# First output chunks in spare PSUM banks, and the last memory head's samples on TensorE

## The chip, the cores and the metric

One core of a Trainium2 chip runs the kernel as one program. The metric is the device time of an execution in microseconds (us), lower is better. A core has five engines that work side by side, each through its own queue in order: PE (TensorE, matmul into PSUM), DVE (VectorE), ACT (ScalarE), POOL (GpSimd) and SP (which here issues the DMAs). PSUM is the memory that matmuls write; this kernel divides it into eight banks of 128 partitions by 512 float32 values.

## What is computed

One inference step of a small decoder with two layers and model width 1024, for a prompt of 256 tokens and 8 samples of one token each, which share the weights; the kernel treats them as 264 columns. Each sublayer f is wrapped as x + norm(f(norm(x))), with an RMS norm whose factor r is one number per column. Layer 0 mixes tokens with a Mamba-2 state-space mixer (SSD), layer 1 with dilated sliding-window attention. After the mixer each layer has cross-attention with 4 heads of 256 dimensions into 256 memory tokens, and a convolutional feed-forward network of width 2816:

```
def cross_attn(u, kv, w_q, w_o):
    n, t_len, _ = u.shape
    q = (u @ w_q).reshape(n, t_len, MEM_HEADS, MEM_HEAD_DIM)
    s = jnp.einsum('nthe,nmhe->nhtm', q, kv[:, :, 0].astype(q.dtype)).astype(jnp.float32) * (MEM_HEAD_DIM ** -0.5)
    p = jax.nn.softmax(s, axis=-1)
    o = jnp.einsum('nhtm,nmhe->nthe', p, kv[:, :, 1].astype(jnp.float32))
    return o.reshape(n, t_len, D_MODEL).astype(u.dtype) @ w_o
```

The prompt's memory keys and values are computed from the memory tokens by weights. Each of the 8 samples has its own memory keys and values, given as a cache (cache_mem_kv). Outputs are the new activations and all new states and caches.

## The kernel before, in words

Activations lie transposed: model dimension on the partitions in chunks of 128, the 264 columns along the free axis. Every weight product is made by `product` (line 771) one output chunk of 128 rows at a time. `wsplit` (757) loads a chunk of weights (tile raw), ACT rounds it to the faster matmul format (hi) and DVE subtracts to get the rest (lo); inputs are split in the same way (uhl). Each of the 8 contraction steps is three matmuls (hi with high input, hi with low input, lo with high input), 24 for a chunk of 8 steps, all into one PSUM accumulator. In `product` the accumulators are the tag "mm" with two banks; raw has four buffers, hi and lo three each.

The eight PSUM banks are divided by tags: mm 2 (products), s 2 (`small`, 716: sums of the norm, the prompt's attention), t 3 (`other`, 719: the samples' work and the state update), f 1 (the memory keys and values and some of the SSD).

A stage begins in `Post.finish` (897): the norm of the sublayer before gives r, then for each of 8 chunks the residual x is updated and split into the next input (`Pre.add`, 875), and its square is summed; `rstd` (801) turns the sum into the next r by a matmul with ones, two ACT operations and three of DVE. The product itself needs only the split input, but the eviction of a query, key, gate or up chunk multiplies by r, so it waits for it: `evac` (798) on DVE in the SSD's conv, the attention's qc and the feed-forward's cons (1679), where a gate chunk then has its convolution (gr, gy) and an up chunk is multiplied with its gate and split (mh, ml). Output products (w_out, xa_o, ffn_d) are evicted by ACT without r.

The memory attention is `xattn` (1313). For each head h it makes two query chunks, then calls `keys` (1348), `soft` (1366) of the head before, `scores` (1394, the prompt's part) and `values` (1381) of the head before. For the samples of one head, `caches` (1326) loads keys or values in four tiles (tag kv, KVB = 6 buffers) of two samples each. For each sample PE broadcasts the query (qs) or the probabilities (prs) over 128 partitions by one matmul into a t bank, and DVE multiplies each of the two halves of the sample's tile with it and sums along the free axis:

```
V.scalar_tensor_tensor(out=kv[:, i, :], in0=kv[:, i, :], scalar=1.0, in1=tq,
                       op0=ALU.mult, op1=ALU.mult, accum_out=a)
```

That is 16 DVE operations (kv<-kv,t in the profile) for the keys of a head and 16 for its values, 128 per layer. `mix` (1421) joins the prompt's result (matmuls s<-ppT,ld with the reloaded prompt values vn) and the samples' (os) into the split input of the output product.

`memkv` (1264) makes the prompt's memory keys and values of a layer in the f bank, stores them (o_memk, o_memv), and `xattn` loads them back. It is called "aside": its operations fill time beside other stages; layer 0's runs beside the output product of the SSD and into the first memory attention, layer 1's up to the second. `states` (1243) updates the SSD states of the samples during the first feed-forward, with t banks.

The order of the instructions on every queue is not that of the source. The program records all operations, and a planner (`Plan.run`, 364, `rank`, `latest` and `order`) lists them with costs of its own: six passes (PASSES) simulate the engines and correct the priorities by the latest times of the pass before; the order with the shortest simulated length is emitted. SPARE sets how early loads are due, SWITCH what a change of ACT's table costs in the choice. A buffer of a tag is given in the order of the source: a later tile of a tag can't have one before an earlier one. All instructions are issued in one line, 622, so the profile's groups are told apart by their tiles.

## Time and profile before

| | us |
|---|---|
| time, median of 3 runs | 1154.57 (1153.74 to 1155.39) |
| the profiled execution, its own time | 1153.77 |
| its span in the profile | 1152.0 |
| PE busy / DVE busy / ACT busy | 1036.8 / 893.9 / 643.8 |

The span is the time from the first to the last instruction that the profiler recorded; the execution's own time has 1.8 us around it. Busy times are those of one engine and overlap with the others'. Matmuls are pipelined: each has a duration of some 0.3 us, but one starts every 0.12 us or so, so the rate is read from the length of a run of them. The stages lie like this in the span (us): SSD 0 to 240, with its output product; first memory attention to 420; first feed-forward to 653; dilated attention to 820; second memory attention to 930; last feed-forward to the end.

### The profile page before, as it was taken

To read this page: it belongs to the slowest core of one execution; us is meant where nothing else is said; L and a number is where in the kernel's file an instruction comes from. 1 tells how busy PE (TensorE), PEld (TensorE's weight loads), DVE (VectorE), ACT (ScalarE), POOL (GpSimd) and SP (SyncE) were. 2 spreads that over 40 slices of the span, in tenths; PEclk is the share of its full clock that TensorE was granted. 3 is DMA by queue.
4 is the path that set the end of the run, shared out by engine and by line. 5 is a ranking of instruction groups with operands and counts; after the bars stand their busy time and mean duration, and the time that the engine had idled before them with its cause. 6 is when DMAs were issued, how large, how long until landed. Compare 5 with 4: busy or idle time off the path is not lost.

```text
span 1152.0 us, 21202 instructions
## 1 busy us (share of the span) xinstructions
PE 1036.8 (90%) x7895; PEld 982.8 (85%) x7895; DVE 893.9 (78%) x2060; ACT 643.8 (56%) x1273; POOL 60.7 (5%) x142
## 2 busy tenths in 40 slices
PE   5899978889998797999999899999884969999995
PEld 5898967889988686999999889989883859999995
DVE  7989999975889889998754675474897776777544
ACT  6896665655643487785544543455542455555542
POOL 0210210000000001221000000000000000000000
PEclk9999989989999798999999999998995989999998
DMA  7335444756799686887566776587398326777761
GB/s 261 128 111 174 158 142 170 258 189 219 263 335 305 233 315 217 306 293 243 173 215 210 251 261 260 192 308 269 128 299 290 118 92 219 284 265 271 271 183 52
DMA packets 80599, 257.20 MB, mean 223 GB/s; under 512 B 16952, under 2 KB 21848, under 8 KB 79344
## 3 DMA queue, kind: packets, MB, share of 16 engines
q1 hardware_dynamic: 80496, 255.85, 64.8%
q8 instruction: 62, 1.02, 0.3%
q14 instruction: 41, 0.34, 0.1%
HBM read 238.70 MB, written 44.34 MB: 246 GB/s over the span
## 4 chain that ended last, share of the span: by engine, by line
PE 63%; DVE 21%; ACT 6%; DMA 5%; issue 4%; SPq 1%; DVEq 0%; ACTq 0%
PE mm L622 48%; PE f L622 6%; PE s L622 6%; DVE kv L622 4%; DVE lo L622 3%; PE t L622 3%; DMA o_sssm<-sto 2%; ACT hi L622 2%; DVE xs L622 1%; DVE hif L622 1%; DVE yv L622 1%; DVE r L622 1%; DVE kvo L622 1%; DVE mix L622 1%; DVE x L622 1%
## 5 line engine op out<-in xcount | busy, mean ns | idle before, releaser
L622 PE MATMUL mm<-uhl,hi 128*128 128x264 f32 x2960 | 574.5, 292 | 41.5 <-ACT uhl L622 14.8
L622 PEld LDWEIGHTS mm<-uhl,hi 128*128 128x128 f32 x2960 | 470.6, 192 | 52.6 <-ACT uhl L622 16.6
L622 DVE TENSOR_TENSOR lo<-raw,hi 128x1024 fp32r<-128x1024 f32 (+1 forms) x283 | 338.7, 1199 | 149.5 <-ACT hi L622 145.7
L622 PE MATMUL mm<-uhl,lo 128*128 128x264 f32 x1480 | 425.0, 288 | 0.7 <-DVE lo L622 0.7
L622 ACT CAST hi<-raw 128x1024 fp32r<-128x1024 f32 (+1 forms) x283 | 292.0, 1033 | 233.5 <-PE mm L622 209.6
L622 PEld LDWEIGHTS mm<-uhl,lo 128*128 128x128 f32 x1480 | 282.6, 191 | 1.7 <-DVE lo L622 1.1
L622 PE MATMUL mm<-mh,lo 128*128 128x264 f32 x352 | 100.1, 284 | 0.0
L622 PE MATMUL mm<-mh,hi 128*128 128x264 f32 x352 | 100.0, 284 | 0.0
L622 PE MATMUL mm<-ml,hi 128*128 128x264 f32 x352 | 99.8, 283 | 0.0
L622 DVE SCALAR_TENSOR_TENSOR kv<-kv,t 128x256 f32<-128x256 f32 x256 | 88.9, 416 | 8.4 <-PE t L622 8.3
L622 PEld LDWEIGHTS mm<-mh,lo 128*128 128x128 f32 x352 | 66.3, 188 | 0.0
L622 PEld LDWEIGHTS mm<-ml,hi 128*128 128x128 f32 x352 | 66.2, 188 | 0.0
L622 PEld LDWEIGHTS mm<-mh,hi 128*128 128x128 f32 x352 | 66.2, 188 | 0.0
L622 PE MATMUL f<-mh,hi 128*128 128x256 f32 x128 | 38.4, 300 | 11.1 <-ACT kvo L622 5.6
L622 ACT ACTIVATE sto<-t,sdt 128x128 f32<-128x128 f32 x128 | 37.3, 394 | 13.4 <-DMA o_sssm<-sto 11.7
L622 DVE SCALAR_TENSOR_TENSOR gy<-gr,ld,gy 128x255 f32<-128x255 f32 x88 | 42.3, 480 | 1.1 <-ACT gy L622 1.0
L622 PE MATMUL f<-hi,mh 128*128 128x256 f32 x128 | 38.4, 300 | 3.2 <-ACT kvo L622 3.2
L622 PE MATMUL f<-ml,hi 128*128 128x256 f32 x128 | 37.4, 292 | 3.8 <-DVE ml L622 3.8
L622 ACT CAST mh<-gy 128x264 fp32r<-128x264 f32 x44 | 18.3, 416 | 39.7 <-DVE gy L622 39.7
L622 PE MATMUL f<-hi,ml 128*128 128x256 f32 x128 | 38.1, 298 | 2.3 <-ACT kvo L622 2.3
L622 POOL COPY pst<-gr 128x2 f32<-128x2 f32 x44 | 23.7, 538 | 304.4 <-DVE gr L622 304.4
L622 PE MATMUL f<-lo,mh 128*128 128x256 f32 x128 | 38.0, 297 | 0.2 <-DVE lo L622 0.2
(284 smaller groups left out, 1717.8 us busy)
## 6 DMA issues: line engine op xcount, KB each, us to landing
raw<-ffn_gu SPq DMA_DIRECT2D x88, 512.0 KB, 4.3
raw<-w_in SPq DMA_DIRECT2D x40, 512.0 KB, 3.5
kv<-cmk SPq DMA_DIRECT2D x32, 512.0 KB, 5.9
kv<-cmv SPq DMA_DIRECT2D x32, 512.0 KB, 5.6
raw<-ffn_d SPq DMA_DIRECT2D x32, 512.0 KB, 3.7
o_sc<-cache SPq DMA_DIRECT2D x16, 1022.0 KB, 8.4
raw<-w_qkv SPq DMA_DIRECT2D x18, 512.0 KB, 3.9
rawf<-state SPq DMA_DIRECT2D x16, 512.0 KB, 4.4
```

What stands on the lines that cost most here:

```text
L622: f(*a, **k)
```

## The change

Three things change. First, `product` takes the bank of its accumulator from a list, head, as long as that has entries: two mm banks, then banks of t or s. The list is set at the start of the program (SSD: five entries), of the dilated attention (five), of the first feed-forward (four: mm, mm, s, s) and of the last (five), and emptied in the memory attention. Entries with 'f' also use the weight buffers of `memkv` (tags rawf, hif, lof, two buffers each). Second, for head 3 (ONPE) of each memory attention the samples' scores and results are made by PE: the 8 samples' queries (or probabilities) are copied by ACT onto the diagonals of a cleared tile dq, so that 32 columns of it hold one sample's query in the column of that sample, and 16 float32 matmuls with such 32 columns as weights and the sample's cache tile as moving operand (256 columns) add up all samples' rows in one bank (`rows_of`). Keys lie transposed in the cache for this head, values as they are. The scores go straight into the soft-max; the values' result is copied and transposed back by PE. Third, the planner tries three values of SPARE with two of SWITCH, four passes each.

```diff
--- before.py
+++ after.py
@@ -28,6 +28,7 @@
 KPOOL = 0
 VPOOL = 0
 KVB = 6
+ONPE = (3,)
 
 
 
@@ -363,14 +364,18 @@
 
     def run(self):
 
-        self.rank()
+        global SPARE, SWITCH
         best = None
-        for i in range(PASSES):
-            self.order(False)
-            if best is None or self.length < best[0]:
-                best = self.length, [o.prio for o in self.ops]
-            self.lengths.append(self.length)
-            self.latest()
+        for SPARE in SPARES:
+            for SWITCH in SWITCHES:
+                self.rank()
+                for i in range(PASSES):
+                    self.order(False)
+                    if best is None or self.length < best[0]:
+                        best = self.length, [o.prio for o in self.ops], SWITCH
+                    self.lengths.append(self.length)
+                    self.latest()
+        SWITCH = best[2]
         if best is not None:
             for o, p in zip(self.ops, best[1]):
                 o.prio = p
@@ -643,6 +648,7 @@
         self.length = max(free.values())
 
 
+BANKS = {"mm": 2, "s": 2, "t": 3, "f": 1}
 SWITCH = 4000.0
 WINDOW = 10240 / 3
 COLUMNS = 3060.0
@@ -665,7 +671,9 @@
 CHANGE = 100.0
 STRETCH = 2.5
 HOLD = 12
-PASSES = 6
+PASSES = 4
+SPARES = 2000.0, 3000.0, 5000.0
+SWITCHES = 2000.0, 4000.0
 SPARE = 3000.0
 COPIES = (0, 1, 2, 0.5, 1)
 SLOTS = 1
@@ -768,14 +776,18 @@
                 E.tensor_tensor(late=LATE_W if late is None else late, out=lo, in0=raw, in1=hi.bitcast(F32), op=ALU.subtract)
             return hi, lo
 
+        head = [('mm', ''), ('mm', ''), ('t', ''), ('t', 'f'), ('t', 'f')]
+
         def product(w, kk, chunks, xh, xl, consume, late=None):
 
             for j in chunks:
-                acc = pm.tile([P, 512], F32, tag="mm", name=nm("mm"), bufs=2)[:, :T]
+
+                tag, own = head.pop(0) if head else ("mm", "")
+                acc = pm.tile([P, 512], F32, tag=tag, name=nm("mm"), bufs=BANKS[tag])[:, :T]
                 wv = w[j].rearrange("p (k c) -> p k c", k=kk)
                 for k0 in range(0, kk, 8):
                     kn = min(8, kk - k0)
-                    hi, lo = wsplit(wv[:, k0:k0 + kn, :], late=late)
+                    hi, lo = wsplit(wv[:, k0:k0 + kn, :], own, (2, 2) if own else (4, 3), late=late)
                     for k in range(kn):
                         PE.matmul(acc, hi[:, k, :], xh[:, k0 + k, :], start=k0 + k == 0, stop=False)
                         PE.matmul(acc, hi[:, k, :], xl[:, k0 + k, :], start=False, stop=False)
@@ -1313,12 +1325,25 @@
         def xattn(l, uh, ul, r):
             with plan.pool("xa%d" % l) as xp:
                 x2 = Two(xp)
+                head[:] = []
                 qT = xp.tile([P, KD, T], F32, name="qT")
                 kT = load(xp, A["o_memk"][l])
                 vn = load(xp, A["o_memv"][l])
                 qs = xp.tile([P, 1024], F32R, name="qs")
                 prs = [xp.tile([P, 256], F32R, name="prs%d" % i) for i in range(2)]
-                zeros(qs, *prs)
+
+                dq = xp.tile([P, 2, 33 * NS], F32, name="dq")
+                zeros(qs, *prs, dq.rearrange("p c a -> p (c a)"))
+                dia = dq.rearrange("p c (n a) -> p c n a", a=33)[:, :, :, 0]
+
+                def rows_of(kv):
+
+                    t = other()
+                    for n in range(NS):
+                        for c in range(2):
+                            PE.matmul(t[0:32, 0:256], dq[:, c, 32 * n:32 * n + 32], kv[n][:, c * 256:c * 256 + 256],
+                                      start=n + c == 0, stop=n == NS - 1 and c == 1)
+                    return t
 
                 def qc(c, acc):
                     evac(qT[:, c, :], acc, r)
@@ -1348,6 +1373,9 @@
                 def keys(h):
 
                     kts = caches(A["cmk"][l, h])
+                    if h in ONPE:
+                        S.copy(dia, qT[:, 2 * h:2 * h + 2, TP:])
+                        return rows_of(kts)
                     t = other()
                     for c in range(2):
                         PE.transpose(t[0:NS, c * P:c * P + P], qT[:, 2 * h + c, TP:], ident)
@@ -1365,9 +1393,12 @@
 
                 def soft(h, sc):
 
-                    t = other()
-                    for mb in range(2):
-                        PE.transpose(t[0:NS, mb * P:mb * P + P], sc[:, mb], ident)
+                    if h in ONPE:
+                        t = sc
+                    else:
+                        t = other()
+                        for mb in range(2):
+                            PE.transpose(t[0:NS, mb * P:mb * P + P], sc[:, mb], ident)
                     mx = x2.tile([NS, 1], F32, tag="mx", name=nm("mx"))
                     V.tensor_reduce(out=mx, in_=t[0:NS, :256], axis=AX.X, op=ALU.max)
                     V.tensor_scalar(out=mx, in0=mx, scalar1=-0.0625, scalar2=None, op0=ALU.mult)
@@ -1376,10 +1407,24 @@
                     S.activation(pr, t[0:NS, :256], AF.Exp, scale=0.0625, bias=mx, accum_out=dn)
                     V.reciprocal(dn, dn)
                     V.tensor_scalar(out=pr, in0=pr, scalar1=dn, scalar2=None, op0=ALU.mult)
-                    stack_rows(prs[h % 2], pr, NS, 32)
+                    if h in ONPE:
+                        t = other()
+                        for mb in range(2):
+                            PE.transpose(t[:, mb * NS:mb * NS + NS], pr[:, mb * P:mb * P + P], ident[0:NS, 0:NS])
+                        S.copy(dia, t[:, 0:2 * NS].rearrange("p (c n) -> p c n", c=2))
+                    else:
+                        stack_rows(prs[h % 2], pr, NS, 32)
 
                 def values(h):
                     vts = caches(A["cmv"][l, h])
+                    if h in ONPE:
+                        t = rows_of(vts)
+                        vr = x2.tile([32, 256], F32, tag="vr", name=nm("vr"), bufs=1)
+                        S.copy(vr, t[0:32, 0:256])
+                        t = other()
+                        for c in range(2):
+                            PE.transpose(t[:, 32 * c:32 * c + 32], vr[:, c * P:c * P + P], ident[0:32, 0:32])
+                        return t[:, 0:64].rearrange("p (c m) -> p c m", c=2)[:, :, 0:NS]
                     os_ = x2.tile([P, 2, NS], F32, tag="os", name=nm("os"), bufs=4)
                     for n in range(NS):
                         vv = vts[n].rearrange("p (c m) -> p c m", c=2)
@@ -1460,6 +1505,7 @@
                 hsel = load(dp, "hsel")
                 hm = load(dp, "hm")
                 qkv = dp.tile([P, 18, T], F32, name="qkv")
+                head[:] = [('mm', ''), ('mm', ''), ('t', ''), ('t', ''), ('t', '')]
                 E.tensor_tensor(late=LATE_V, out=rope, in0=rope, in1=r.unsqueeze(1).to_broadcast([P, 2, T]), op=ALU.mult)
 
                 def qc(c, acc):
@@ -1675,6 +1721,7 @@
                 mh = fp.tile([P, KF, T], F32R, name="mh")
                 ml = fp.tile([P, KF, T], F32R, name="ml")
                 gate = {}
+                head[:] = [('mm', ''), ('mm', ''), ('t', ''), ('t', 'f'), ('t', 'f')] if l else [('mm', ''), ('mm', ''), ('s', ''), ('s', '')]
 
                 def cons(c, acc):
                     if c < KF:
@@ -1842,11 +1889,11 @@
     def tra(a):
         return a.T.reshape(2, P, 256).transpose(1, 0, 2).reshape(P, 512)
 
-    def heads(a, f):
-        return np.stack([np.stack([np.stack([f(a[l, n, :, h]) for n in range(NS)], axis=1)
+    def heads(a, f, g):
+        return np.stack([np.stack([np.stack([(g if h in ONPE else f)(a[l, n, :, h]) for n in range(NS)], axis=1)
                                    for h in range(4)]) for l in range(2)])
-    o["cmk"] = heads(i["cache_mem_kv"][:, :, :, 0], nat)
-    o["cmv"] = heads(i["cache_mem_kv"][:, :, :, 1], tra)
+    o["cmk"] = heads(i["cache_mem_kv"][:, :, :, 0], nat, tra)
+    o["cmv"] = heads(i["cache_mem_kv"][:, :, :, 1], tra, nat)
     for g, (nmc, st) in enumerate((("cache_swa_kv_w128", 1), ("cache_swa_kv_w512", 4), ("cache_swa_kv_w2048", 16))):
         c = i[nmc][0]
         o["cache%d" % g] = c.reshape(NS, c.shape[1], 2, 256)
```

## Rows read from the trace of the kernel before

**Rows 1.** The page, part 1: busy us, share of the span, instructions.

```profile
PE 1036.8 (90%) x7895; PEld 982.8 (85%) x7895; DVE 893.9 (78%) x2060; ACT 643.8 (56%) x1273; POOL 60.7 (5%) x142
```

**Rows 2.** The page, part 4: the chain that ended last, by engine.

```profile
PE 63%; DVE 21%; ACT 6%; DMA 5%; issue 4%; SPq 1%; DVEq 0%; ACTq 0%
```

**Rows 3.** Windows by stage: us, each engine busy, granted clock, DMA share, GB/s.

```profile
62.00:240.00 178.00, 157.36 (x1207) 143.43 (x1207) 173.16 (x339) 121.98 (x233) 17.76 (x28) 0.97 0.51 167
315.00:400.00 85.00, 71.47 (x473) 65.30 (x472) 75.33 (x308) 33.92 (x80) 0.00 (x0) 0.90 0.84 294
434.00:513.00 79.00, 70.96 (x545) 68.26 (x545) 75.42 (x126) 62.33 (x148) 14.83 (x20) 0.96 0.79 268
859.00:907.00 48.00, 28.83 (x135) 21.71 (x134) 40.70 (x210) 11.79 (x33) 0.00 (x0) 0.72 0.66 229
955.50:1139.00 183.50, 183.50 (x1516) 183.50 (x1516) 119.92 (x195) 93.30 (x140) 9.39 (x42) 1.00 0.67 234
```

**Rows 4.** Timeline of PE where a feed-forward's third chunk starts: start, us, [idle <-releaser].

```profile
450.60 0.81 PE L622 MATMUL mm<-uhl,hi 128*128 128x264 f32 x2 [5.99 <-DVE gr L622]
...
950.45 0.81 PE L622 MATMUL mm<-uhl,hi 128*128 128x264 f32 x2 [5.38 <-DVE gr L622]
```

**Rows 5.** The chain that ended last, a run of product matmuls: start, us, count.

```profile
910.51 17.56 PE mm L622 x143
```

**Rows 6.** Windows at the stages' starts, columns as in rows 3.

```profile
934.30:945.10 10.80, 10.21 (x52) 8.62 (x52) 9.70 (x27) 5.99 (x16) 0.00 (x0) 0.81 0.01 2
945.10:950.45 5.35, 0.00 (x0) 0.00 (x1) 3.90 (x6) 2.56 (x5) 0.00 (x0) 0.83 0.30 98
950.45:955.50 5.05, 5.05 (x23) 5.05 (x24) 1.87 (x5) 2.71 (x4) 0.31 (x2) 0.50 0.33 104
444.60:450.60 6.00, 0.01 (x1) 0.00 (x1) 6.00 (x10) 4.10 (x12) 0.00 (x0) 0.69 0.82 270
18.66:22.54 3.88, 0.00 (x1) 0.04 (x1) 3.81 (x7) 1.24 (x3) 0.00 (x0) 1.00 1.03 373
653.00:660.00 7.00, 6.45 (x50) 6.18 (x51) 7.00 (x20) 5.36 (x14) 0.00 (x0) 1.00 0.88 316
```

**Rows 7.** Timeline of DVE, the last feed-forward's first gate chunk.

```profile
949.96 0.43 DVE L622 TENSOR_TENSOR gr<-mm,r 128x264 f32<-128x264 f32 x1
...
951.07 0.48 DVE L622 SCALAR_TENSOR_TENSOR gy<-gr,ld,gy 128x255 f32<-128x255 f32 x1 [0.68 <-ACT gy L622]
```

**Rows 8.** The page, part 5: count, busy us, mean ns, idle before.

```profile
L622 DVE SCALAR_TENSOR_TENSOR kv<-kv,t 128x256 f32<-128x256 f32 x256 | 88.9, 416 | 8.4 <-PE t L622 8.3
```

**Rows 9.** Timeline of PE, float32 matmuls (two records each).

```profile
320.64 1.99 PE L622 MATMUL s<-ld,qT 128*128 128x256 f32 x8 [0.98 <-DMA ld<-o_memk]
...
726.42 2.59 PE L622 MATMUL t<-swk,qe 128*32 128x128 f32 x22
```

**Rows 10.** Timelines of DVE and ACT, tail of the second memory attention.

```profile
863.42 0.42 DVE L622 TENSOR_TENSOR qT<-mm,r 128x264 f32<-128x264 f32 x1
...
874.09 0.42 DVE L622 SCALAR_TENSOR_TENSOR kv<-kv,t 128x256 f32<-128x256 f32 x1 [1.78 <-PE t L622]
...
896.84 0.41 DVE L622 TENSOR_REDUCE mx<-t 8x1 f32<-8x256 f32 x1
...
898.46 0.34 DVE L622 TENSOR_SCALAR pr<-pr,dn 8x256 f32<-8x256 f32 x1
...
907.25 0.20 ACT L622 CAST uhl<-os 128x16 fp32r<-128x16 f32 x1 [3.44 <-DVE kv L622]
```

**Rows 11.** Timeline of SP: issues of loads.

```profile
380.22 0.38 SPq L622 DMA_DIRECT2D ld<-o_memv  x1
...
875.57 1.70 SPq L622 DMA_DIRECT2D kv<-cmk  x2
```

**Rows 12.** Tile kv, 820 to 895 us: how long its loads take.

```profile
DMA to landing us min/median/max: 3.6/5.5/8.0
```

**Rows 13.** Timeline of PE: the first matmuls with the reloaded values, first memory attention.

```profile
391.00 4.24 PE L622 MATMUL s<-ppT,ld 128*128 128x256 f32 x16
```

## The prediction

> **What bounds the kernel now.** I read the page's busy line first: TensorE (PE) is busy 90% of the span, VectorE (DVE) 78%, ScalarE (ACT) 56% [rows 1], and the chain that ended last is 63% PE and 21% DVE [rows 2]. So the kernel is near TensorE's limit, but not everywhere. The windows by stage show where [rows 3]: the last feed-forward runs PE without a hole (183.50 of 183.50 us), while the SSD stage is DVE's (173.16 of 178), the first feed-forward up to 513 us is DVE's too (75.42 of 79), and the end of the second memory attention, 859 to 907 us, has PE busy 28.83 of 48 us at a mean granted clock of 0.72, with DVE at 40.70. A PE microsecond saved counts in full only where PE is full afterwards; one added costs nothing only where it is idle.
>
> Two kinds of hole matter. At the start of a stage, PE fills its two accumulators while the normalised input arrives and then stands still until the norm's factor r lets DVE evict them: 5.38 us before the last feed-forward's third chunk, 5.99 us before the first's, both released by DVE's eviction gr [rows 4]. The other is the tail of the memory attention, where DVE's row products kv follow one another.
>
> **The added banks, stage by stage.** One weight chunk is 24 matmuls of 264 columns; 143 such matmuls took 17.56 us at the full clock, so 0.123 us each and 2.95 us a chunk [rows 5].
>
> Last feed-forward: between 934.30 and 955.50 us, PE started 52 + 0 + 23 = 75 matmuls [rows 6], four of them for the norm's sum, so 71 of the product. With five banks it has 120 to do before it needs an eviction, that is 14.8 us. The clock granted there is 0.81 up to 945.10, and 0.19 x 10.8 = 2.1 us are lost to it; with 0.5 us for the norm's sum, five chunks end at 934.3 + 17.4 = 951.7, past the first eviction near 950. So the gap closes, and with it the stretch at 0.50, which is 1.2 GHz, that follows it. By 955.5 PE would have done (21.2 - 2.6) / 0.123 = 151 instead of 71: 80 x 0.123 = 9.8 us. The least is the idle gap alone, 5.35. I take **9.0**, since some input chunks arrive late; PE is full from there to 1139 [rows 3], so it is kept. The five weight chunks must have been split (ACT rounds, DVE subtracts) by 943; the change gives two of them buffers of their own, and DVE's subtractions of 1.2 us fit ahead of 930, where DVE is not full.
>
> Five full banks have to be drained once r exists. Chunks three to five are two gates and an up; a gate takes DVE an eviction of 0.43 us and two multiply-adds of 0.48 [rows 7], an up its eviction and a subtraction of much the same size, about 3.6 us in all. I cost it at nothing: the first eviction alone frees the bank that PE needs next, and DVE is busy 119.92 of the 183.50 us behind it [rows 3]; if that cover fails, 9.0 becomes 5.4. The Trainium skill's page "PSUM — Partial Sum Buffer", section "Summary: rules for kernel authors", says "Evacuate promptly — 2 MiB is tight", and banks held full until r exists go against that. By that rule 9.0 would fall to 5.4; the trace, with DVE a third idle there, does not bear it out.
>
> First feed-forward: the extra banks are those of the small work, of which one still holds the norm's sum; one chunk (2.95 us) fits surely into the 5.99, a second perhaps. But DVE is busy 6.00 of 6.00 us in that gap [rows 6] and stays so up to 513, feeding the state update. Ends 0 and 6.0; I take **3.0**, the one chunk. SSD: the hole is 3.88 us, but DVE is busy 3.81 of it [rows 6] and 97% of the stage. Ends 0 and 3.9; I take **0.5**. Dilated attention: memory-key matmuls fill its start already, 6.45 of 7.00 us [rows 6]. Ends 0 and 0.55; I take **0.5**.
>
> **The last head on TensorE.** Removed per layer: 32 kv operations on DVE, 88.9 / 256 = 0.347 us each [rows 8], so 11.1 us, 16 broadcast matmuls of 256 columns on PE (about 0.12 us each by [rows 5], 1.9 us), four transposes and two stacked casts. Added per layer: 32 float32 matmuls with 32 stationary and 256 moving columns, each two records. Eight records of 128 x 256 took 1.99 us, and 22 of a 32-column stationary with 128 columns took 2.59 us, 0.118 each with the last one's drain [rows 9]; so about 0.222 a record at 256 columns, 14.2 us for 64, and two blocks of 7.1. Net PE +12.3 us per layer, 24.6 in all; the four small transposes and copies balance those removed. The clearing of the diagonal tile is one DVE instruction per layer, a part of a microsecond beside the norm. The loads stay as they are in number and size.
>
> The Trainium skill's page "TensorE: Matmul & The Clock Gate", section "Why this matters for your kernels", has several 32-column matmuls running side by side if their outputs lie at different partitions. Four at a time would make the 14.2 us 3.6. Here all outputs lie at partitions 0 to 31, and the row of the 32-column matmuls shows the full price, so I keep 14.2.
>
> Second memory attention. By 863.42 the last query chunk is evicted; after that DVE ran five kv blocks (keys 2, values 1, keys 3, values 2, values 3), with a wait for the soft-max's way through PE and ACT ahead of some (1.78 us before 874.09), until ACT splits the last result at 907.25 [rows 10]. Without head 3 three blocks remain, and head 3 is a chain of its own: its last keys are issued at 875.57, when values 1 frees their buffers, and the last of the two 1.7 us later [rows 11]; a load lands 5.5 us after issue (3.6 to 8.0) [rows 12], so about 883; the last tile's eight records take 1.8 us: 885. The soft-max took from 896.84 to 898.80 [rows 10], with transposes and copies 3 us: 888. The last values' buffer comes free at 885, lands at 891, 1.8 us of matmuls: 893; copy, transposes, split 2 us: 895. That is 12 us before 907.25. PE's own work: 28.83 us busy in 48, or 20.8 if all ran at the mean clock, plus 12.3, makes 33 to 41 us from 859: 892 to 900, a gain of 7 to 15. DVE falls from 40.70 to 29.6 and bounds nothing. I take **10.5**, between the chain and the PE bound's middle.
>
> First memory attention. DVE gives up the same 11.1 us, but there the prompt's values of this layer are still being made: their reload is issued at 380.22 [rows 11] and the first matmul that reads it starts at 391.00 [rows 13], with at most 8.0 us of it the load. Head 3 finished earlier is then late on nothing; the reload is next. Best case 391.0 - 388.2 = 2.8 us; worst, the 7.1 us key block stands ahead of the value matmuls on PE's in-order queue and delays the reload by that much. PE has 85 - 71.47 = 13.5 us idle in this stage [rows 3], which holds the added 12.3. Ends -7.1 and +2.8; I take **0**.
>
> The planner now picks among 24 orders instead of 6, by its own model; every queue's order (PE, ACT, DVE, POOL and SP's loads) may move. No row prices that. The nearest are the starts' holes of 5.4 and 6.0 us, which one badly placed wait can make or remove: ends -6 and +6, I take **0**.
>
> **Sum.** 9.0 + 3.0 + 0.5 + 0.5 + 10.5 = 23.5 us. The profiled execution took 1153.77 us (span 1152.0), 0.8 below the median 1154.57; 1154.6 - 23.5 = **1131**.
>
> **The rivals.**
> (a) Only the starts pay. The tail of layer 1 stays as long, because its loads, six buffers deep, come as late as before, or PE puts the float32 blocks late. For it: SP issues each load only when a buffer is freed [rows 11]. Against: fewer blocks wait for DVE. 1131 + 10.5 = 1142.
> (b) The splits of chunks three to five come too late, so the extra banks don't fill: one chunk more per feed-forward, 2 x 2.95 = 5.9, with the tail: 1154.6 - 16.4 = 1138. For it: DVE is full ahead of the first feed-forward. This is also the case that the change does not do what it says.
> (c) The backlog of evictions in the last feed-forward: 3.6 us given back, 1135. This is where the PSUM page's rule would lead; DVE's slack speaks against it.
> (d) Slower: the float32 blocks on PE. If the order puts them before work that others wait for (the value matmuls of layer 0, the output product), they aren't hidden in idle time. It decides once more than the 13 us that the starts save stay uncovered of 24.6; with all of it 1154.6 + 11.6 = 1166, the middle about 1160. For it: PE is 90% busy, and its queue is in order, so a block that waits for its last load, or for ACT's copy of the query into the diagonal, holds up every matmul behind it. Against: 13.5 and 19.2 us idle in just the two stages that take the blocks.
>
> **How the numbers follow.** Forecast 0.53; (a) 0.18; (b) 0.08; (c) 0.05; (d) 0.10; gains and costs that cancel 0.06. About 0.2% (2.3 us) is what a measurement of this kernel can tell from no change. Faster 0.84, same 0.06, slower 0.10. The range reaches down by the upper ends of layer 1 (4.5), the first feed-forward (3), SSD (3.4) and layer 0 (2) to 1118, and up past (a) and (b) with a misplaced wait of 6 to 1149; (d) is left out.
>
> **What would show it.** Right: no idle over 2 us on PE before gr in the last feed-forward and half as much in the first; kv operations on DVE down from 256 to 192; in the second memory attention ACT's last split at most 37 us after the last query eviction, instead of 43.8, at a higher granted clock; PE busy up by less than the added 24.6 us. Wrong: the waits for gr remain; the second memory attention's tail keeps its 44 us; or the first memory attention lengthens by 5 us or more.

## The result: 1139.4 us, a gain of 15.5 where 23.5 was forecast

The changed kernel takes **1139.44 us** (median of 4, 1137.92 to 1141.24) against 1154.98 for the kernel before beside it: ratio 0.9855, 95% interval 0.9829 to 0.9882 (the ratios are those on record; they can differ from the quotient of two medians by up to 0.2%). That is faster, by an interval that excludes no change, and inside the range of 1118 to 1149. How the gain comes about is another matter: the experiments give the banks more than the forecast did, and head 3 on TensorE no gain instead of 10.5 us, by the medians a loss of some 4, which in the whole change is not clear of noise.

The page of the kernel after, parts 1 and 4 and the kv line of part 5:

```profile
PE 1051.8 (93%) x7991; PEld 987.9 (87%) x7991; DVE 868.4 (76%) x1930; ACT 647.2 (57%) x1277; POOL 61.7 (5%) x142
...
PE 66%; DVE 17%; ACT 7%; DMA 6%; issue 3%; SPq 0%; DVEq 0%; ACTq 0%
...
L627 DVE SCALAR_TENSOR_TENSOR kv<-kv,t 128x256 f32<-128x256 f32 x192 | 66.9, 415 | 4.8 <-PE t L627 3.3
```

Against [rows 1, 2, 8]: DVE does 64 kv operations fewer, its busy time falls by 25.5 us, PE's rises by 15.0, and PE's idle time, span less busy, falls from 115.2 to 84.3. The span fell by 15.9, which is 30.9 less idle minus 15.0 more work. The kernel is now more nearly all PE.

The timeline of PE after, where the two feed-forwards start: the wait for gr in the first, and the first product matmuls of the last.

```profile
458.63 0.48 PE L627 MATMUL mm<-uhl,hi 128*128 128x264 f32 x2 [0.82 <-DVE gr L627]
...
926.95 1.47 PE L627 MATMUL mm<-uhl,hi 128*128 128x264 f32 x5 [4.13 <-ACT uhl L627]
```

The 5.99 us before gr [rows 4] are 0.82, and the 5.38 us in the last feed-forward are gone; the wait of 4.13 us for the norm's own input is as long there as it was before, at 934.32. In the SSD stage the hole of 3.88 us [rows 6] is gone too, but PE waits 6.15 us for DVE a little later, at 39.12, and the stage is no shorter. To compare stages, cut every trace where a stage's norm first writes mix on DVE, so that a stage holds its whole output product. Lengths in us of one profiled execution each; f is the number of memory-key and memory-value matmuls (tile f) that PE did in the stage, from windows on that tile:

| kernel | SSD | attn 1 | ffn 1 | dilated | attn 2 | ffn 2 | f by stage |
|---|---|---|---|---|---|---|---|
| before | 284.0 | 146.6 | 220.8 | 159.6 | 121.6 | 210.9 | 96, 384, 88, 169, 84 |
| after | 287.3 | 146.5 | 216.7 | 154.5 | 120.1 | 202.0 | 96, 384, 71, 138, 131 |
| banks alone | 284.9 | 142.9 | 214.3 | 152.7 | 126.3 | 202.2 | 96, 360, 70, 129, 165 |
| banks, repeat | 285.1 | 142.9 | 213.9 | 157.1 | 126.5 | 202.0 | 96, 360, 71, 128, 166 |
| head alone | 290.4 | 146.6 | 220.7 | 161.0 | 122.0 | 210.6 | 96, 384, 95, 164, 83 |

### The profile page after: what moved, and what is told of

Same layout as the page of the kernel before. It is cut to its first block, busy times and chain, and to the rows that moved or that the text cites. A ratio compares the mean times of both kernels' runs of the same rounds, so it can differ in the third digit from the quotient of the medians.

```text
span 1136.1 us, 21248 instructions
## 1 busy us (share of the span) xinstructions
PE 1051.8 (93%) x7991; PEld 987.9 (87%) x7991; DVE 868.4 (76%) x1930; ACT 647.2 (57%) x1277; POOL 61.7 (5%) x142
## 4 chain that ended last, share of the span: by engine, by line
PE 66%; DVE 17%; ACT 7%; DMA 6%; issue 3%; SPq 0%; DVEq 0%; ACTq 0%
PE mm L627 46%; PE f L627 7%; PE s L627 7%; PE t L627 5%; DVE lo L627 3%; DVE kv L627 2%; DMA o_sssm<-sto 2%; ACT hi L627 2%; DVE kvo L627 2%; DVE xs L627 1%; ACT kvo L627 1%; ACT L602 1%; DVE hif L627 1%; DVE yv L627 1%; DMA raw<-xa_o 1%
## 5 line engine op out<-in xcount | busy, mean ns | idle before, releaser
L627 PEld LDWEIGHTS mm<-uhl,hi 128*128 128x128 f32 x2960 | 469.0, 191 | 38.3 <-ACT uhl L627 15.9
L627 DVE SCALAR_TENSOR_TENSOR kv<-kv,t 128x256 f32<-128x256 f32 x192 | 66.9, 415 | 4.8 <-PE t L627 3.3
L627 DVE SCALAR_TENSOR_TENSOR gy<-gr,ld,gy 128x255 f32<-128x255 f32 (+1 forms) x88 | 42.0, 480 | 2.8 <-ACT gy L627 2.6
L627 PE MATMUL mm<-gh,hi 128*128 128x264 f32 x128 | 36.9, 291 | 4.2 <-ACT gh L627 3.2
L627 PE MATMUL mm<-gh,lo 128*128 128x264 f32 x128 | 37.6, 294 | 0.0
```

The lines of the kernel that those rows point to most:

```text
L627: f(*a, **k)
```

## Experiments

**1. Take the change apart.** Four kernels: only the banks, only the head, only the planner's search, and everything but the search.

```diff
 e1_banks_only
-ONPE = (3,)
+ONPE = ()
 e2_pe_only: no lists of banks
-        head = [('mm', ''), ('mm', ''), ('t', ''), ('t', 'f'), ('t', 'f')]
+        head = []
...
-                head[:] = [('mm', ''), ('mm', ''), ('t', ''), ('t', ''), ('t', '')]
+                head[:] = []
...
 e3_planner_only: both edits
 e4_old_planner
-PASSES = 4
-SPARES = 2000.0, 3000.0, 5000.0
-SWITCHES = 2000.0, 4000.0
+PASSES = 6
+SPARES = 3000.0,
+SWITCHES = 4000.0,
```

> Only the banks (and the new search of the planner); head 3 stays on DVE. Theory A (the banks pay by filling the starts of the two feed-forwards, the last head on PE pays some 5 to 7 us more by moving work off DVE): last feed-forward 8 to 9 us shorter than before, first 2 to 4, in all 1141 to 1146. Rival B (the last head on PE pays nothing, its PE work eats what DVE saves): as fast as the full change, 1137 to 1141. Rival C (the gain is the planner's search): about the full change too, but then the planner alone gives it as well.

> Only head 3's samples on PE (and the new search); every product accumulates in the two mm banks. Theory A: 1146 to 1151, with the memory attentions shorter and the waits for gr back at 5 to 6 us. Rival B: 1154 to 1160, since 24.6 us of PE work are added to a PE that is 90% busy. Rival C: about 1140, with the waits for gr still there.

> The kernel before with the new search of the planner alone (three values of SPARE, two of SWITCH, four passes). Theory A: within 3 us of before, 1151 to 1157, and if anything it carries the longer SSD stage. Rival C: 1148 or less.

> Banks and head 3 on PE, with the planner's search as before (one SPARE, one SWITCH, six passes). Theory A: 1135 to 1143. Rival C: 1146 or more. If the SSD stage is back at 284 us to its last output chunk's norm (287 with the full change), its loss belongs to the order found by the new search; if not, to the banks there.

| kernel | us | ratio to before | interval |
|---|---|---|---|
| banks alone | 1135.72 | 0.9818 | 0.979 to 0.9847 |
| head alone | 1161.18 | 1.0045 | 1.0026 to 1.0063 |
| search alone | 1156.67 | 0.9998 | 0.9977 to 1.0019 |
| all but the search | 1140.01 | 0.9846 | 0.9797 to 0.9894 |

The banks alone give 20 us, more than the whole change. The head alone is slower, by an interval that excludes no change. The search does nothing: the instruction order with it alone is that of before on every engine, and without it that of the changed kernel, so the last row is a second measurement of the change. The profiled executions of that one order differ by 5.7 us (spans 1136.1 and 1130.4), so single spans tell less than the medians. Stages differ in this: the second memory attention repeats within 0.2 us (119.9 in the second profile of the change, 126.3 and 126.5 with the banks alone), while the dilated attention does not (154.5 and 151.4; 152.7 and 157.1).

The head alone gains nothing in the two attentions that it changes, and loses next to nothing: 146.6 and 122.0 us against 146.6 and 121.6. Its loss lies in the SSD stage, ahead of both, which takes 290.4 instead of 284.0 (experiment 3).

**2. Why the banks pay more: lists taken away.** In the table the banks (the repeat) leave 24, 17 and 41 of the f matmuls undone in three stages, and the second memory attention does them, 82 more, for only 4.9 us. The dilated attention shows the exchange at its start: of the 167 matmuls that PE ran in its first 25 us, 80 were f before; with the banks alone 51 of 184. Two tests: the list of the last feed-forward alone (no f left to move there), and all lists but the dilated attention's.

```diff
 e5_last_ffn_banks (head 3 on DVE)
-        head = [('mm', ''), ('mm', ''), ('t', ''), ('t', 'f'), ('t', 'f')]
+        head = []
...
-... if l else [('mm', ''), ('mm', ''), ('s', ''), ('s', '')]
+... if l else []
 e6_no_attn_banks (head 3 on DVE)
-                head[:] = [('mm', ''), ('mm', ''), ('t', ''), ('t', ''), ('t', '')]
+                head[:] = []
```

> Head 3 on VectorE as before, the list of banks in the last feed-forward stage alone. There no memory-key block is left to move, so the gain is the stage's own: in the runs so far that stage was 8.7 to 8.9 us shorter than before (210.9 to 202.0 and 202.2), and the forecast's term was 9.0. Theory: about 1146 to 1147 us, and the stages ahead of it as before within 2 us, the memory-key blocks placed as before (96, 384, 88, 169, 84 by stage). Rival: the shorter stage is paid for by starts further up, then it is under 3 us shorter with this list alone, about 1152.

> Head 3 on VectorE, the lists in the SSD stage and in both feed-forward stages, none in the dilated attention. Theory (a start that is filled with products leaves its memory-key blocks to the second memory attention, where TensorE waits for VectorE): the dilated attention goes back from 152.7 to about 158 us and takes about 165 memory-key blocks again instead of 129, the second memory attention gets about 35 fewer and, as TensorE idles there, shortens by only 1 to 2 us: about 1139 to 1141. The forecast's term for this list, 0.5 us, would make it 1136, the same as with all lists and head 3 on VectorE (1135.7).

The last list alone: 1144.31 us, ratio 0.9906 (0.988 to 0.9933); its stage 202.1 us instead of 210.9, the stages ahead within 1.7 us of before and their f as before. The median's 11.4 us is over the stage's 8.8, and the interval holds both. That rival falls.

Without the attention's list: 1143.47 us, ratio 0.991 (0.9878 to 0.9943), 7.8 us over all lists. Its f is some 173 in the dilated attention and 109 in the second memory attention, as the theory had it, but the time is longer than either number on record, and the comparison is not clean: the planner gave this kernel another order of the SSD stage, 288.2 us instead of 285. Taking off those 3.2 leaves 4.6 for the list, against 0.5 forecast; the interval of this kernel's ratio alone is 3.7 us to either side, so 4.6 is an estimate. The stage itself, windows of the profile (columns as in [rows 3]), without the list and, at the same granted clock, of a kernel with it (e11 below; head 3 differs only behind this stage):

```profile
650.90:819.00 168.10, 164.22 (x1168) 151.27 (x1167) 99.87 (x253) 74.89 (x175) 0.00 (x0) 0.90 0.69 247
```

```profile
643.50:802.50 159.00, 156.12 (x1124) 143.85 (x1123) 96.51 (x252) 72.47 (x173) 0.00 (x0) 0.90 0.69 249
```

44 matmuls and 9.1 us lie between the two. The matmuls are the memory work that the list pushes out of a stage where PE is full; at 0.12 us each they are 5 to 6 us. The rest of the 9.1 is not explained, and the profiled execution without the list, 1154.73 us, was 11 us over its kernel's median. In the order of before, without the list, three profiled executions took 159.6, 163.8 and 160.1 us in this stage (before, the search alone, the last list alone), in the banks' order four took 152.7, 157.1, 154.0 and 159.0 (e1, e12, e9, e11). Where the memory work goes, PE was waiting, as windows of before show over the second memory attention's tail, from the last query eviction to the last split and behind it:

```profile
863.50:888.00 24.50, 10.80 (x39) 6.93 (x38) 21.09 (x112) 4.69 (x16) 0.00 (x0) 0.57 0.89 312
888.00:907.30 19.30, 16.88 (x90) 14.13 (x90) 15.48 (x78) 5.63 (x17) 0.00 (x0) 0.84 0.30 99
907.30:932.60 25.30, 21.01 (x163) 19.64 (x161) 14.75 (x22) 14.62 (x27) 0.60 (x1) 0.98 0.51 168
```

and with the banks alone (the repeat):

```profile
852.10:876.00 23.90, 17.26 (x113) 14.79 (x111) 22.18 (x106) 9.31 (x20) 0.00 (x0) 0.93 0.93 322
876.00:900.60 24.60, 18.63 (x91) 15.98 (x92) 19.37 (x93) 6.86 (x19) 0.00 (x0) 0.72 0.46 159
900.60:925.50 24.90, 20.49 (x161) 19.43 (x159) 14.33 (x22) 14.45 (x26) 0.92 (x1) 0.99 0.53 173
```

In the first 24 us PE ran 39 matmuls at a granted clock of 0.57, and 113 at 0.93 with the moved work in the gaps: 74 more in no more time.

**3. Is the head's loss the SSD stage's order?** In the head alone the SSD stage, whose code is untouched, is 6.4 us longer. e7 gives its operations the priorities of the plan without head 3 on PE.

```diff
+        for o, p in zip(plan.ops[:plan.mark], ref.ops[:ref.mark]):
+            o.prio = p.prio
```

> Head 3 on TensorE, no lists, and the instructions of the SSD stage keep the priorities that the plan gives them without head 3 on TensorE. Theory (the work on TensorE costs what it saves, and part of the loss is the order that the planner finds for the SSD stage): the SSD stage is 284 to 285 us instead of 290.4, and the whole about 1155 to 1156, level with before. Rival (all of the loss is the price of the blocks on TensorE and the rest only moved): it stays at 1160 to 1161, and what the SSD stage gets back is lost behind it.

1161.88 us, ratio 1.0047 (1.0025 to 1.0069). By the numbers this is nearer the rival: the SSD stage is 287.5 us, 2.9 less than in the head alone, and the first memory attention (148.8) and the first feed-forward (224.9) take it back. But it is no clean test. The priorities do not fix the order: PE's queue parts from that of before some 61 us into the SSD stage. The other kernels answer for that stage. Those whose SSD order is that of before or of the banks alone have 283.7 to 285.1 us, with head 3 on PE among them (e8, e9, e11: 284.4, 284.2, 285.0); those with another order have 287.1 to 290.4, with head 3 on DVE among them (e6: 288.2). So 2 to 3 us in the changed kernel, and 6 in the head alone, come with the order that the planner happens on for a stage in which the head has no work.

**4. Make the head's products cheap.** e8 is the whole change with the samples' rows at four groups of 32 partitions instead of one, so that four products can lie side by side; the transposes and copies follow, and the planner's cost for such a product is set to 120 ns.

```diff
-                            PE.matmul(t[0:32, 0:256], dq[:, c, 32 * n:32 * n + 32], ...
+                            for j in range(4):
+                                n = 2 * j + i
+                                PE.matmul(t[32 * j:32 * j + 32, 0:256], dq[:, c, 32 * n:32 * n + 32], ...
```

> The whole change, but the samples' rows of head 3 are written at four groups of 32 partitions, so that four of the 32-column float32 products can lie side by side in TensorE's array. In the SSD stage of the kernel before, 64-column float32 products to two halves of the partitions took 0.053 us each, those of 32 columns to one place 0.111. If four run side by side, a block of 32 records takes about 2 to 3.5 us instead of 7.1, TensorE is busy some 8 to 10 us less in the second memory attention, and, if the price of the head on TensorE is that time, the whole comes to 1128 to 1134 us, under that with the lists alone (1135.7). Rivals: they don't overlap, then 1139 to 1140 as with the whole change; or they do and the stage still waits for VectorE's other three heads, then 1136 to 1139 with TensorE idle in the gain's place.

The products do run side by side. PE's timeline, after and then tiled:

```profile
873.31 3.64 PE L627 MATMUL t<-kv,dq 128*32 128x256 f32 x16 [0.87 <-DVE kv L627]
...
886.67 7.09 PE L627 MATMUL t<-kv,dq 128*32 128x256 f32 x32
```

```profile
873.34 1.92 PE L630 MATMUL t<-kv,dq 128*32 128x256 f32 x26
...
886.06 2.07 PE L630 MATMUL s<-ppT,ld 128*128 128x256 f32 x4 [1.45 <-DMA ld<-o_memv]
```

0.074 us a record instead of 0.222, both at a granted clock of 1.00; 26 records of the value block took 2.84 us, at 0.66. And yet 1141.28 us, ratio 0.9877 (0.9848 to 0.9905), no better than the change (0.9855). So the products' own time does not set this kernel's length. It is no clean pair with the change either: from 46 us on PE's order is another, and the second memory attention takes 129.3 us with 144 f in it. The second row shows what is late there: the prompt's products wait for memory values that were written to DRAM and read back. The last f matmuls start 75.7 us into the stage, in the changed kernel 56.0.

**5. One attention at a time.** ONPE becomes pairs of layer and head. e9 is instruction for instruction the banks alone up to the second memory attention, so nothing ahead of it differs; e10 is the changed kernel up to there, and PE keeps its order even up to the first product of head 3, 873.31 us in the changed kernel. e11 is e9 with tiled products, e12 the banks alone again.

```diff
-ONPE = (3,)
+ONPE = ((1, 3),)      e9, e11 (tiled)
+ONPE = ((0, 3),)      e10
```

> The lists alone once more, beside the three kernels that are to be compared with it on one chip: 1134 to 1138 us, 20 us under the kernel before.

> All lists, and head 3 on TensorE in the second memory attention only. Every instruction up to that attention is the same, in the same order, as with the lists alone, so the order found for the SSD stage and the first memory attention can't blur this pair. Theory (the loss of the head sits in the SSD stage's order and in the first memory attention, where TensorE has no idle time that it saves, and the second attention gains the 6.2 us by which it was shorter in the whole change than with the lists alone, 120.1 against 126.3): 1128 to 1131 us. Rival (its products take as long on TensorE as the wait that they end, and the 6.2 us are the 34 memory-key blocks that the whole change had placed earlier): the same as the lists alone within 2 us.

> All lists, and head 3 on TensorE in the first memory attention only. Up to the second attention its instructions stand as in the whole change. Against the lists alone it carries the other order of the SSD stage (2.4 us in the profiles) and the first attention's price (142.9 to 146.5). If the second attention's gain is real this is the slowest of the four: 1142 to 1145 us. If the second attention gains nothing: 1139 to 1140, as the whole change.

> As the one with head 3 on TensorE in the second memory attention only, but with its products at four groups of partitions (26 of them took 1.9 and 2.8 us in the profile of the first kernel that did so, against 7.1 us for 32). If TensorE's time in the second attention sets its end, 5 to 9 us less than without the tiling, 1121 to 1126. If the values of the last memory rows do, which are written to DRAM and read back before the prompt's heads can use them (in that first kernel: written from 873.97, read from 876.73, and the prompt's products waited until 886.06), nothing is gained by it: equal within 2 us.

| kernel | us | ratio | interval | attn 1 | attn 2 |
|---|---|---|---|---|---|
| banks alone (e12) | 1135.51 | 0.9836 | 0.9817 to 0.9856 | 142.9 | 126.5 |
| head, second attention (e9) | 1139.96 | 0.9878 | 0.9859 to 0.9897 | 142.7 | 130.0 |
| the same, tiled (e11) | 1137.70 | 0.9848 | 0.982 to 0.9876 | 142.7 | 126.5 |
| head, first attention (e10) | 1141.00 | 0.9876 | 0.9853 to 0.9899 | 147.4 | 122.3 |

e9 against e12 has the same order ahead, the same 165 f in the stage, and intervals that do not meet. The head costs 4.4 us by the medians, 3.5 in the stage. That is worse than the rival's "within 2 us", and the theory on record (1128 to 1131) falls. Within the stage the pair is not clean: PE's order is another from 21 us into it, and the last f matmuls start 81 us into it instead of 72. e10 against the changed kernel is the closer pair, and there the head gains: 120.1 us with it, 122.3 without, 131 f in both. By the medians (1139.44 and 1141.00, from two sets) the intervals overlap. So the head's worth in this attention has no sign of its own; it changes with the order, and with the memory work that stands in the same stage. Windows of e9 over the same stretches as e12's above:

```profile
850.80:875.00 24.20, 20.52 (x112) 15.08 (x112) 17.83 (x82) 7.38 (x19) 0.00 (x0) 0.86 0.91 325
875.00:898.20 23.20, 19.37 (x102) 13.52 (x101) 11.80 (x46) 7.80 (x19) 0.00 (x0) 1.00 0.49 172
898.20:926.60 28.40, 25.17 (x200) 24.26 (x198) 14.92 (x23) 15.16 (x27) 0.33 (x1) 0.99 0.45 149
```

From the last query to the samples' last split it takes 47.4 us, against 48.5: DVE is relieved (29.6 us busy instead of 41.6), but PE is as late. Behind the split it has 200 matmuls to do instead of 161, 28.4 us instead of 24.9: the 3.5 us. Of those 39, four are value products of the prompt and 35 are output products, which in e12 ran ahead of the split. Two things come later in e9. The first is the memory values: the last of them are written and read back, first in e12, then in e9, by the issues of SP:

```profile
872.51 0.34 SPq L627 DMA_DIRECT2D o_memv<-kvo  x1
...
877.53 0.39 SPq L627 DMA_DIRECT2D ld<-o_memv  x1
```

```profile
879.16 0.34 SPq L627 DMA_DIRECT2D o_memv<-kvo  x1
...
882.41 0.42 SPq L627 DMA_DIRECT2D ld<-o_memv  x1
```

And PE's timeline, where the prompt's last value products and the first output products start, again e12 and then e9:

```profile
885.73 7.83 PE L627 MATMUL s<-ppT,ld 128*128 128x256 f32 x24
...
895.63 0.47 PE L627 MATMUL mm<-uhl,hi 128*128 128x264 f32 x1
```

```profile
867.22 3.64 PE L627 MATMUL t<-kv,dq 128*32 128x256 f32 x16
...
871.65 3.64 PE L627 MATMUL t<-kv,dq 128*32 128x256 f32 x16
...
882.62 5.37 PE L627 MATMUL t<-kv,dq 128*32 128x256 f32 x24 [0.28 <-ACT dq L627]
...
888.84 1.91 PE L627 MATMUL t<-kv,dq 128*32 128x256 f32 x8 [0.85 <-DMA kv<-cmv]
...
891.35 6.31 PE L627 MATMUL s<-ppT,ld 128*128 128x256 f32 x28 [0.60 <-DMA ld<-o_memv]
...
898.61 0.59 PE L627 MATMUL mm<-uhl,hi 128*128 128x264 f32 x2
```

In e9 the two halves of the key block, 7.3 us, stand among the last f matmuls. Although the stage began 2.4 us earlier than in e12, the last memory values leave 6.7 us later, are read back 4.9 later, and the prompt's value products start 5.6 later, released by that DMA. The second is the head's value block: it stands right ahead of them in PE's queue, up to 890.75, so that they wait only 0.60 us for the DMA. The output products begin at 898.61, after the split; in e12 they began 5 us ahead of it. Which of the two would hold them alone, the read-back or the block, was not tried.

Tiling (e11) gains 2.3 us by the medians, but the intervals overlap; in the profile it takes back the stage's 3.5 us, and it stays short of the 5 to 9 that PE's time alone would give. e10, by its stages, puts the first attention at 4.5 us over the banks alone, of which about 3 are 25 more f (0.12 us each) that it does earlier, so some 1.5 are left for the head. That it is slower than the whole change is not resolved: 0.9876 against 0.9855 with intervals that overlap.

The best kernel measured is therefore the banks alone: 1135.5 and 1135.7 us in two sets, below both kernels. Against the change itself the intervals overlap; against e9 they do not.

## Why the prediction was right, and where its steps were not

**Last feed-forward, 9.0.** Right: the stage lost 8.9 us in the changed kernel, 8.8 with this list alone and 7.8 to 8.9 in all that have it, and the wait for gr is gone. The cover for the backlog of evictions held: ff 2 is as short as the sum made it, so rival (c) is out, and with the closed gap (b).

**First feed-forward, 3.0; dilated attention, 0.5.** Too small: 4.1 in the changed kernel (7.0 in its second profile) and 5.0 to 6.9 with the banks' order for the first, of which some 2 are 17 f left for later; about 4.6 for the second, by the estimate of experiment 2. The step that failed is "memory-key matmuls fill its start already, 6.45 of 7.00 us". The row is misread, since it counts all of PE's matmuls: of those 50 only 19 are f, 3.17 us. And I took a filled start as having nothing to gain. But those matmuls have no date in that stage; products that take their place push them on, up to the second memory attention, where PE was waiting at a clock of 0.57. Counted over the kernel, the lists' gain is about 20 us instead of 13.

**SSD, 0.5.** Nothing gained: 1 us longer with the banks alone, 3.3 in the changed kernel, which is within what the planner's order does to the stage. No run has this list alone. The hole is closed, but PE waits for DVE later, as the lower end of this term had it.

**Second memory attention, 10.5.** Wrong in size everywhere, and in sign in one of the orders: the stage grows by 3.5 us with the banks' order and by 0.4 for the head without lists, and shrinks by 2.2 with the changed kernel's order (e10 against after). Two sub-steps held: a block took 7.09 us where 7.1 was worked out, and the samples' tail shortened, to 38.4 us in the changed kernel (857.81 to 896.21) from 43.8, at a granted clock of 0.91 instead of 0.69. The timeline of ACT after, its last rows:

```profile
893.80 0.36 ACT L627 COPY vr<-t 32x256 f32<-32x256 f32 x1 [6.11 <-PE t L627]
...
896.21 0.18 ACT L627 CAST uhl<-t 128x16 fp32r<-128x16 f32 x1
...
897.89 0.59 ACT L627 CAST uhl<-s 128x512 fp32r<-128x512 f32 x1 [1.50 <-PE s L627]
```

It fell by 5.4 and not by 12. From the last query, the key block ended after 23.3 us where 21.6 were worked out, the soft-max's copy came 3.1 late, and the value block ended after 36.0 instead of 29.6. Half of this is the value block: I let 24 of its 32 records overlap with the loads, and they started only after the soft-max's copy, all 32 in a row at 886.67 (experiment 4). Nor do the samples end the tail any more, which the chain did not foresee. The last row is the prompt's split, 40.1 us after the last query, over the 37 that was to be the sign of being right; before it came at 903.23, ahead of the samples' at 907.25. Its value products stand behind the head's block in PE's queue:

```profile
893.70 1.99 PE L627 MATMUL s<-ppT,ld 128*128 128x256 f32 x8
...
895.86 1.99 PE L627 MATMUL s<-ppT,ld 128*128 128x256 f32 x8
```

The larger error is that I priced the last split as if it were the stage's end. The output products that ran ahead of it were cover that the head's blocks consumed: behind the split stand 28.9 us in the changed kernel and 25.3 before. So 3.6 of the 5.4 come back, and the stage is 1.5 us shorter, with 47 more f in it than before. Windows of the changed kernel from the last query to the next stage, to be held against before's in experiment 2:

```profile
857.90:882.00 24.10, 17.91 (x94) 12.17 (x93) 19.47 (x90) 8.71 (x24) 0.00 (x0) 0.86 0.94 329
882.00:896.30 14.30, 14.30 (x70) 9.27 (x69) 6.74 (x36) 3.52 (x10) 0.00 (x0) 1.00 0.47 184
896.30:925.20 28.90, 25.72 (x202) 24.70 (x200) 15.54 (x23) 15.25 (x29) 0.33 (x1) 1.00 0.45 148
```

PE is without a hole for the last 14 us ahead of the split, and 202 matmuls follow it instead of 163. My window from 859 to 907 did hold the idle PE time, 19.2 us, but I counted it for the head alone, while the moved memory work wanted it too.

**First memory attention, 0.** Within the ends, on the side of a loss: e10 gives +4.5 over the banks alone, some 1.5 of it for the head; the head without lists 0.0, in e7's order 2.2. From e12 to e10 what lies idle on PE there fell from 18.2 to 8.8 us while its work rose by 13.9 (124.7 to 138.6).

**Planner, 0.** Right for the search: same order. The other part, that any edit can move the order, was worth 2 to 3 us in the SSD stage of the changed kernel, within my 6, and 6.4 in the head alone.

**Rivals.** (a), only the starts pay, comes nearest by mechanism and was given 1142. (d) has its number in the head alone, slower by 0.45%, but not its reason, since that loss lies in the order of the SSD stage. What (d) describes, a block ahead of work that others wait for, is seen in the second attention, where the prompt's value products stand behind the block of 7.09 us. It did not decide the whole because the lists gave 20 us and not 13. So the time fell inside the range by luck as much as by the sum: two errors of opposite sign, 7 us too little for the banks and some 14 too much for the head with the order that came with it.

## What to carry to other kernels

Work without a date that fills a hole does not make the hole worthless: ask where that work goes when something better takes its place, and whether the engine waits there. When a wait near a stage's end is shortened, count what ran ahead inside it, since that must now run behind. Change one part at a time: here one of three parts paid for everything, one paid nothing (and cost 4.4 us in one of the orders tried) and one did nothing, and the sum alone could not have told. Where a planner makes the order, an edit in one stage can lengthen another that it does not touch, so compare stages whose order is the same.

## What the hardware showed that I had not expected

Float32 products of 32 columns whose outputs lie at four groups of partitions took 0.074 us a record against 0.222 with all at one group, three times as fast (rows in experiment 4). What was expected of e8 put a block at 2 to 3.5 us instead of 7.1; that this gains next to nothing for the kernel is what I had not expected. The Trainium skill, page "TensorE: Matmul & The Clock Gate", section "Why this matters for your kernels", has several such products side by side; the trace agrees, with a factor of three for four groups here at the full granted clock.

The granted clock differs between executions of one and the same program. The dilated attention with the banks alone, in its two profiled executions:

```profile
642.10:794.80 152.70, 149.94 (x1124) 137.67 (x1123) 96.51 (x251) 72.28 (x173) 0.00 (x0) 0.94 0.72 261
```

```profile
641.90:799.00 157.10, 154.40 (x1124) 142.27 (x1124) 96.56 (x252) 72.51 (x173) 0.00 (x0) 0.91 0.71 252
```

The same 1124 matmuls, and 4.4 us between them, as much as the head's price in e9. Two more executions of this order (e9 and e11) took 154.0 us at 0.93 and 159.0 at 0.90: the lower the granted clock, the longer the stage. A difference of that size between two profiles is no evidence by itself; the medians and stages that repeat are.
